# Splitting h into its two float32r parts where it is made, on one Trainium2 core

## The chip, the core and the metric

The kernel is written in the Tile language (dependences, buffer waits and the order of instructions on each engine come from its scheduler) and runs on one NeuronCore of a Trainium2 chip. The metric is the device time of one execution in microseconds (us). TensorE is PE in the rows, its weight loads PEld, VectorE DVE, ScalarE ACT, GpSimd POOL, SyncE SP; SP issues nearly all DMAs, in its own order.

## What is computed

One layer of a hybrid backbone over 2048 latent tokens and 256 context tokens of width 1024. The modulated norm h of all tokens goes through one input projection, whose columns feed three token mixers:

```python
hl = modulate(rms_norm(xl, p["norm_mix_pre"]), ml[0], ml[1])
hc = modulate(rms_norm(xc, p["norm_mix_pre"]), mc[0], mc[1])
qkv_l, z_l, beta_l, alpha_l, lx_l, lg_l, rw_l = split_last(hl @ p["w_in"], IN_SIZES)
qkv_c, z_c, beta_c, alpha_c, lx_c, lg_c, rw_c = split_last(hc @ p["w_in"], IN_SIZES)
```

The mixers are a gated DeltaNet (`gdn`), an RG-LRU (`lru`) and RWKV-7 (`rwk`), each scanned in both directions. Their concatenated outputs go through an output projection, a residual and a squared-ReLU MLP. All is float32. The kernel reaches that accuracy on TensorE with float32r products: an operand x is split into hi = float32r(x) and lo = x - hi, and a product is hi*hi + lo*hi + hi*lo, three matmuls.

## The kernel before

h is made once and kept in DRAM as a float32 tensor `ht` of [128, 8, 2312]: 128 features by 8 groups by the padded tokens. The tokens come in nine pieces of 256 (piece 0 is the context), which overlap by a few columns for the convolutions; a pass over a piece reads 260 columns (`PW`).

`make_h` (L286) makes it, two tiles of 128 tokens to a piece. For each tile x is loaded ("mhx", two buffers), ScalarE squares it into an "mhh" tile (two buffers) to get the row sum, VectorE makes the reciprocal root in some fifteen tiny steps (`rms`), GpSimd scales x (L315), TensorE transposes it in two halves `q` of four 128x128 blocks into PSUM tiles of the tag "rps", ScalarE and VectorE apply scale and shift into the same mhh tile, and SP writes it to `ht` (L328). The pieces come in the order `H_ORDER` = 0, 1, 2, 8, 7, 3, 6, 4, 5. Three are emitted ahead of the RWKV sweep, two in its first piece and one in each of the next four, behind the norm of k (L838).

`Proj.load` (L387) reads a pass: per unit of `u` feature groups a DMA of `ht` into a "hl" tile (L394), a ScalarE cast to hi, "hh" (L397), and a GpSimd subtraction for lo in a second "hl" tile (L398). `Proj.products` (L414) issues the three matmuls (tile "proj"), and `weight` uses the same "hl" ring to stage the weights. There are 54 passes: 9 in the RWKV sweep (u=2, six buffers of each name), 27 in the gated-DeltaNet features (u=2, eight buffers), 9 each in `lru_features` and `gdn_gates` (u=4, three hh and four hl buffers).

The stages: `front` holds make_h and `rwkv_sweep` (L757), which per piece projects 12 column tiles (x3, k, v, r), then for each direction makes decay and in-context rate with small matmuls of the same PSUM tag "rps" (w_up, a_up, evicted as lw and ta), a VectorE scan and products, and writes `pk`. `mixed` weaves the RWKV recurrence with `gdn_features`; `rest` weaves the gated-DeltaNet recurrence with `lru_features`, the LRU, `gdn_gates` and the output projection; `ffn` is last. The program is written in this order, and the scheduler places each engine's instructions by its own model of their times.

Of the kernel before, what the change touches and what calls it, by code (L numbers as in the profile page):

```python
# [7 lines left out]
F32 = mybir.dt.float32  # L8
F32R = mybir.dt.float32r
# [8 lines left out]
KD = 8  # L18
# [4 lines left out]
PW = 260  # L23
# [20 lines left out]
def poff(p):  # L44

    return 0 if p == 0 else 259 + 256 * (p - 1)
# [1 line left out]


SCRATCH = {  # L50
    "ht": ([128, KD, HPAD], F32),
    "modc": ([128, 2, KD], F32),
    "gp2": ([128, D], F32),
    "kq": ([2, 128, NCH, 2, 3, 64], F32),
# [231 lines left out]
def make_h(k, w, pp, tag):  # L286

    d = k.d
    zf = w.tile([128, KD, 4], F32, name="zf", bufs=1)
    k.G.memset(zf, 0.0)  # L290
    k.S.dma_start(out=d["ht"][:, :, 0:2], in_=zf[:, :, 0:2])
    k.S.dma_start(out=d["ht"][:, :, 258:261], in_=zf[:, :, 0:3])
    k.S.dma_start(out=d["ht"][:, :, 2309:2312], in_=zf[:, :, 0:3])

    def load(p):
        xt = []
        for i in range(2):
            t = w.tile([128, D], F32, name="mhx", bufs=2)
            src = d["ctx"][0, 128 * i:128 * i + 128, :] if p == 0 else \
                d["x"][0, 256 * (p - 1) + 128 * i:256 * (p - 1) + 128 * i + 128, :]  # L300
            k.S.dma_start(out=t, in_=src)
            xt.append(t)
        return xt

    for n, p in enumerate(H_ORDER):
        xt = load(p)
        if n == 0:
            yield
        j = 1 if p == 0 else 0
        sc, sh = k.sc[:, j], k.sh[:, j]  # L310
        for i, x in enumerate(xt):
            h = w.tile([128, KD, 128], F32, name="mhh", bufs=2)
            rs = w.tile([128, 1], F32, name="mhs", bufs=6)
            k.act(h.rearrange("p a t -> p (a t)"), x, AF.Square, acc=rs)
            k.ts(k.G, x, x, k.rms(w, rs, D, 1e-6), MUL)  # L315
            for q in range(2):
                ps = pp.tile([128, 4, 128], F32, name="mhps", tag=tag)
                for a in range(4):
                    kk = 4 * q + a
                    k.PE.transpose(ps[:, a, :], x[:, 128 * kk:128 * kk + 128], k.ident)  # L320
                for a in range(4):
                    kk = 4 * q + a
                    if a < 3:
                        k.act(h[:, kk, :], ps[:, a, :], AF.Identity, scale=sc[:, kk:kk + 1], bias=sh[:, kk:kk + 1])
                    else:
                        k.ts(k.V, h[:, kk, :], ps[:, a, :], sc[:, kk:kk + 1], MUL, sh[:, kk:kk + 1], ADD)
            o = poff(p) + 2 + 128 * i
            k.S.dma_start(out=d["ht"][:, :, o:o + 128], in_=h)  # L328
        yield


# [9 lines left out]
class Proj:  # L341


    def __init__(self, k, es, tag, psb=2, u=4, hb=3, raw=4, side="right"):
        self.k, self.u, self.lb, tc = k, u, raw, k.tc
        self.w = es.enter_context(tc.tile_pool(name=tag + "w", bufs=1, side=side))
        self.hp = es.enter_context(tc.tile_pool(name=tag + "h", bufs=hb, side=side))
        self.pp = es.enter_context(tc.tile_pool(name=tag + "p", bufs=psb, space=PSUM, side=side))
        self.nw = 0

    def weight(self, i, c0, m):

        k = self.k
        self.hi[i], self.lo[i] = [self.w.tile([128, KD, m], F32R, name=f"w{x}{i}") for x in ("hi", "lo")]
        n = 2 * self.u
        for q in range(0, KD, n):
            s = slice(q, q + n)
            split(k, (k.V, k.G)[i % 2], k.d["w_in"][0, 128 * q:128 * (q + n), c0:c0 + m].rearrange("(k p) f -> p k f", p=128),
                  self.raw(F32).rearrange("p a t -> p (a t)")[:, 0:n * m].rearrange("p (k f) -> p k f", f=m),
                  self.hi[i][:, s, :], self.lo[i][:, s, :])  # L360

    def raw(self, dtype):

        return self.hp.tile([128, self.u, PW], dtype, name="hl", bufs=self.lb)

    def weights(self, cols):

# [18 lines left out]

    def load(self, p):  # L387

        k = self.k
        out = []  # L390
        o = poff(p)
        for q in range(0, KD, self.u):
            raw, hh, hl = self.raw(F32), self.hp.tile([128, self.u, PW], F32R, name="hh"), self.raw(F32R)
            k.S.dma_start(out=raw, in_=k.d["ht"][:, q:q + self.u, o:o + PW])  # L394
            for a in range(0, self.u, 2):
                x = slice(a, a + 2)
                k.A.copy(hh[:, x, :], raw[:, x, :])  # L397
                k.tt(k.G, hl[:, x, :], raw[:, x, :], hh[:, x, :], SUB)  # L398
            out.append((hh, hl))
        return out  # L400

    def parts(self, f, h, a=0, b=PW):
# [10 lines left out]

    def products(self, ps, f, h, kk, a, b):  # L414

        hh, hl = h[kk // self.u]
        m = self.hi[f].shape[2]
        for n, (w, x) in enumerate(((self.hi[f], hh), (self.hi[f], hl), (self.lo[f], hh))):
            self.k.mm(ps[0:m, 0:b - a], w[:, kk, :], x[:, kk % self.u, a:b], kk == 0 and n == 0, kk == KD - 1 and n == 2)

    def feats(self, fs, h, a=0, b=PW):

# [48 lines left out]
def gdn_features(k, es, sm):  # L471

    d, tc, V, A, G = k.d, k.tc, k.V, k.A, k.G
    cw = k.pc["gdn_conv"]
    c4 = lambda v: v.rearrange("p r (n t) -> p r n t", t=64)
    pj = Proj(k, es, "g", u=2, hb=8, raw=8)
    w = es.enter_context(tc.tile_pool(name="gfw", bufs=2, side="right"))
    gt = chain(gates(k), decays(k, sm))
    rest = ada_rest(k, es.enter_context(k.tc.tile_pool(name="adr", bufs=1, side="right")), sm, "sm")

    def rows(p, y, a):
        to_rows(k, sm, w, d["kv"][0, :, 4 * p:4 * p + 4, a, :], y, "gsq")

    def normed(p, y, sq, s):

        scale = 64.0 if s else 1.0
        k.table("natural_log_exp_and_others")
        for a, b in ((0, 2), (2, 3)):
# [12 lines left out]
        if s == 0:  # L501
            k.tt(G, y, y, sq, MUL)
            rows(p, y, 0)
            yield

    before = None
    tiles = lambda c: [(c + 128 * j, 128) for j in range(3)]
    for s, p, h in pj.passes([tiles(GW) + [(C_BA, 24)], tiles(0), tiles(2 * GW)]):
        next(rest, None)
        y = w.tile([128, 3, 256], F32, name="gy")  # L510
        f0 = (3, 0, 6)[s]
        for j in range(3):
            ps = yield from pj.parts(j, h)
            k.act(y[:, j, :], ps[:, 0:256], AF.Copy, scale=cw[:, f0 + j:f0 + j + 1])
            for tap in range(1, 4):
                k.stt(y[:, j, :], ps[:, tap:tap + 256], cw[:, 9 * tap + f0 + j:9 * tap + f0 + j + 1], y[:, j, :], MUL, ADD)
            yield
        if s == 0:
            ps = yield from pj.parts(3, h, 2, 258)
            b = w.tile([24, 256], F32, name="gba", bufs=1)  # L520
            V.tensor_copy(b, ps[0:24, 0:256])
            k.S.dma_start(out=d["ba"][:, 256 * p:256 * p + 256], in_=b)
        if before:
            yield from normed(*before)
            before = None
        if s > 0:
            next(gt, None)
            next(gt, None)
        k.table("silu_and_others")
        k.act(y, y, AF.Silu)  # L530
        if s < 2:
            sq = w.tile([128, 3, 256], F32, name="gsq", bufs=1)
            k.tt(G, sq, y, y, MUL)
            before = p, y, sq, s
        else:
            rows(p, y, 1)
# [361 lines left out]
def front(k):  # L898

    with ExitStack() as es:  # L900
        pj = Proj(k, es, "r", psb=3, u=2, hb=6, raw=6, side="left")
# [956 lines left out]
```

## Time and profile before

| | us |
|---|---|
| median of 3 runs (lowest to highest) | 4217.18 (4215.35 to 4218.16) |
| profiled execution, own time | 4210.2 |
| its span, first to last instruction | 4208.5 |
| TensorE matmul busy | 3591.0 (85%) |
| VectorE busy | 2424.2 (58%) |
| GpSimd busy | 1672.0 (40%) |
| ScalarE busy | 1574.5 (37%) |
| mean granted TensorE clock, share of full | 0.89 |

Busy time is that of the profiled execution. Matmuls overlap in the array, so a TensorE busy for 90% of a stretch may still have room. "Idle before" of a group of instructions is the time that the engine stood idle just ahead of them, with what ended it. The chain of waits is followed back from the last instruction, at each step to what released it.

### The profile page before, as it was taken

To read this page: it belongs to the slowest core of one execution; us is meant where nothing else is said; L and a number is where in the kernel's file an instruction comes from. 1 tells how busy PE (TensorE), PEld (TensorE's weight loads), DVE (VectorE), ACT (ScalarE), POOL (GpSimd) and SP (SyncE) were. 2 spreads that over 40 slices of the span, in tenths; PEclk is the share of its full clock that TensorE was granted. 3 is DMA by queue.
4 is the path that set the end of the run, shared out by engine and by line. 5 is a ranking of instruction groups with operands and counts; after the bars stand their busy time and mean duration, and the time that the engine had idled before them with its cause. 6 is when DMAs were issued, how large, how long until landed. Compare 5 with 4: busy or idle time off the path is not lost.

```text
span 4208.5 us, 75743 instructions
## 1 busy us (share of the span) xinstructions
PE 3591.0 (85%) x29914; PEld 2997.3 (71%) x29914; DVE 2424.2 (58%) x4389; ACT 1574.5 (37%) x3163; POOL 1672.0 (40%) x1589
## 2 busy tenths in 40 slices
PE   5798995888778867587787689989999999999998
PEld 2777774777667756576675467768888887888886
DVE  3566667766757543299979985643334346333334
ACT  3454443444454532232564445532222222211212
POOL 3333334444465543355585645322232214212212
PEclk8998996788988777788798679999999999999999
DMA  7433335344555644543454556631212123111112
GB/s 207 126 110 121 117 110 170 108 136 135 163 158 158 179 125 148 148 123 110 133 164 146 159 174 186 202 116 46 66 57 62 56 73 125 55 46 46 54 42 85
DMA packets 491798, 499.09 MB, mean 119 GB/s; under 512 B 38819, under 2 KB 443956, under 8 KB 491444
## 3 DMA queue, kind: packets, MB, share of 16 engines
q1 hardware_dynamic: 477620, 471.18, 37.6%
q0 software_dynamic: 5120, 16.78, 1.4%
q10 hardware_dynamic: 8704, 6.29, 0.5%
q8 instruction: 237, 3.88, 0.4%
q14 instruction: 117, 0.96, 0.1%
HBM read 368.45 MB, written 136.30 MB: 120 GB/s over the span
## 4 chain that ended last, share of the span: by engine, by line
PE 50%; DVE 22%; DMA 14%; issue 5%; ACT 5%; POOL 2%; SPq 2%; DVEq 0%; ACTq 0%; POOLq 0%
PE fup L161 16%; PE fdn L161 16%; PE proj L161 6%; PE opm L161 4%; DVE yl L135 3%; DVE ltmp L135 3%; DMA hl<-ht 3%; DMA pk<-pk 3%; PE rps L161 2%; DMA ht<-mhh 2%; DVE ml L1115 1%; DVE pk L135 1%; PE gps L161 1%; DMA dm<-gb 1%; DVE y L1138 1%
## 5 line engine op out<-in xcount | busy, mean ns | idle before, releaser
L161 PE MATMUL proj<-hh,whi 128*128 128x258 f32 (+2 forms) x2040 | 642.4, 318 | 67.0 <-ACT hh L397 17.5
L161 PE MATMUL proj<-hl,whi 128*128 128x258 f32 (+2 forms) x2040 | 627.3, 308 | 3.4 <-POOL hl L135 3.4
L161 PE MATMUL proj<-hh,wlo 128*128 128x258 f32 (+2 forms) x2040 | 623.0, 306 | 0.0
L135 DVE TENSOR_TENSOR facc<-facc,fdn 128x512 f32<-128x512 f32 x480 | 326.3, 686 | 399.0 <-PE fdn L161 399.0
L161 PEld LDWEIGHTS proj<-hh,whi 128*128 128x128 f32 x2040 | 417.3, 206 | 100.4 <-issue 42.1
L161 PEld LDWEIGHTS proj<-hl,whi 128*128 128x128 f32 x2040 | 420.4, 206 | 20.9 <-issue 9.6
L161 PEld LDWEIGHTS proj<-hh,wlo 128*128 128x128 f32 x2040 | 418.7, 206 | 15.9 <-issue 11.3
L135 POOL TENSOR_TENSOR hl<-hl,hh 128x520 fp32r<-128x520 f32 x216 | 296.5, 1379 | 305.1 <-ACT hh L397 235.6
L161 PE MATMUL fup<-fhh,uhi 128*128 128x512 f32 x1024 | 404.5, 395 | 5.7 <-ACT fhh L336 5.7
L161 PE MATMUL fup<-fhl,uhi 128*128 128x512 f32 x1024 | 403.5, 394 | 2.7 <-DVE fhl L135 2.5
L161 PE MATMUL fup<-fhh,ulo 128*128 128x512 f32 x1024 | 403.2, 394 | 0.0
L161 PE MATMUL fdn<-dhi,ah 128*128 128x512 f32 x1024 | 399.7, 391 | 3.8 <-ACT ah L1758 2.0
L161 PE MATMUL fdn<-dlo,ah 128*128 128x512 f32 x1024 | 399.6, 390 | 0.2 <-POOL dlo L135 0.2
L161 PE MATMUL fdn<-dhi,al 128*128 128x512 f32 x1024 | 395.4, 391 | 0.9 <-DVE al L135 0.9
L135 POOL TENSOR_TENSOR dlo<-draw,dhi 128x1024 fp32r<-128x1024 f32 x32 | 77.5, 2422 | 564.2 <-ACT dhi L336 564.2
L336 ACT CAST dhi<-draw 128x1024 fp32r<-128x1024 f32 x64 | 67.1, 1049 | 576.8 <-PE fdn L161 515.0
L135 POOL TENSOR_TENSOR fq<-fr 128x512 f32<-128x512 f32 x128 | 151.8, 1187 | 326.1 <-ACT fr L113 325.4
L397 ACT CAST hh<-hl 128x520 fp32r<-128x520 f32 x216 | 131.3, 623 | 280.9 <-DMA hl<-ht 274.2
L161 PEld LDWEIGHTS fup<-fhh,uhi 128*128 128x128 f32 x1024 | 192.7, 188 | 51.1 <-ACT fhh L336 7.5
L161 PEld LDWEIGHTS fup<-fhl,uhi 128*128 128x128 f32 x1024 | 192.8, 188 | 48.3 <-DVE fhl L135 4.4
L161 PEld LDWEIGHTS fdn<-dhi,ah 128*128 128x128 f32 x1024 | 192.3, 188 | 48.2 <-DVE facc L135 3.0
L135 DVE TENSOR_TENSOR al<-fq,ah 128x512 fp32r<-128x512 f32 x128 | 93.6, 732 | 229.9 <-ACT ah L1758 229.5
(368 smaller groups left out, 7894.8 us busy)
## 6 DMA issues: line engine op xcount, KB each, us to landing
hl<-ht SPq DMA_DIRECT2D x144, 260.0 KB
uraw<-in_ffn_up_dram SPq DMA_DIRECT2D x64, 512.0 KB
draw<-in_ffn_down_dram SPq DMA_DIRECT2D x64, 512.0 KB
pk<-pk SPq DMA_DIRECT2D x18, 1536.0 KB
pk<-pk SPq DMA_DIRECT2D x36, 768.0 KB
hl<-ht SPq DMA_DIRECT2D x36, 520.0 KB
pb<-pk SPq DMA_DIRECT2D x36, 384.0 KB
kqe<-kq SPq DMA_DIRECT2D x72, 192.0 KB
```

Source lines behind the costliest of these rows:

```text
L135: return e.tensor_tensor(out=out, in0=a, in1=b, op=op)
L161: self.last = self.PE.matmul(out, l, r, start=start, stop=stop).ins
L336: k.A.copy(hi, raw)
L397: k.A.copy(hh[:, x, :], raw[:, x, :])
L1115: V.transpose(out=sw(ml[part]), in_=mu[part, :, cc].rearrange("p u i -> p i u"))
L1138: V.transpose(out=y[part, :, cc].rearrange("p u i -> p i u"), in_=sw(yl[part]))
```

## The change

`ht` gets a further axis of two, hi and lo, and its size doubles. make_h now writes each half `q` of a token tile into an mhh tile of its own, [128, 4, 2, 128] float32r (4 KB per partition, as a whole tile had before; still two buffers under one name): the shifted value goes into the lo place, ScalarE copies it rounded into the hi place, GpSimd subtracts in place, and SP writes that half. `Proj.load` becomes one DMA per unit, straight into what the matmuls read; the rings "hh" and "hl" become one ring "hx" of `hb` units of both parts. The matmuls are the same.

```diff
-    "ht": ([128, KD, HPAD], F32),
+    "ht": ([128, KD, 2, HPAD], F32),
...
         for i, x in enumerate(xt):
-            h = w.tile([128, KD, 128], F32, name="mhh", bufs=2)
+            hs = [w.tile([128, 4, 2, 128], F32R, name="mhh", bufs=2)]
             rs = w.tile([128, 1], F32, name="mhs", bufs=6)
-            k.act(h.rearrange("p a t -> p (a t)"), x, AF.Square, acc=rs)
+            k.act(hs[0].bitcast(F32).rearrange("p a b t -> p (a b t)"), x, AF.Square, acc=rs)
             k.ts(k.G, x, x, k.rms(w, rs, D, 1e-6), MUL)
...
+                if q == 1:
+                    hs.append(w.tile([128, 4, 2, 128], F32R, name="mhh", bufs=2))
+                h = hs[q]
+                whole = h[:, :, 1, :].bitcast(F32)
...
-            k.S.dma_start(out=d["ht"][:, :, o:o + 128], in_=h)
+                k.A.copy(h[:, :, 0, :], whole)
+                k.tt(k.G, h[:, :, 1, :], whole, h[:, :, 0, :], SUB)
+                k.S.dma_start(out=ht[:, 8 * q:8 * q + 8, o:o + 128], in_=h.bitcast(F32).rearrange("p k a t -> p (k a) t"))
...
+    def unit(self):
+        return self.hp.tile([128, self.u, 2, PW], F32R, name="hx")
...
         for q in range(0, KD, self.u):
-            raw, hh, hl = self.raw(F32), self.hp.tile([128, self.u, PW], F32R, name="hh"), self.raw(F32R)
-            k.S.dma_start(out=raw, in_=k.d["ht"][:, q:q + self.u, o:o + PW])
-            for a in range(0, self.u, 2):
-                x = slice(a, a + 2)
-                k.A.copy(hh[:, x, :], raw[:, x, :])
-                k.tt(k.G, hl[:, x, :], raw[:, x, :], hh[:, x, :], SUB)
-            out.append((hh, hl))
+            x = self.unit()
+            self.k.S.dma_start(out=x.bitcast(F32).rearrange("p k a t -> p (k a) t"),
+                               in_=self.k.d["ht"][:, q:q + self.u, :, o:o + PW].rearrange("p k a t -> p (k a) t"))
+            out.append(x)
```

## Rows read from the trace of the kernel before

**Rows 1.** busy time of each engine by stage; columns named in the first line

```profile
core 0: us, PE busy (x) PEld busy (x) DVE busy (x) ACT busy (x) POOL busy (x), PEclk, DMA share, GB/s
78.00:631.00 553.00, 483.54 (x3105) 424.61 (x3107) 346.54 (x724) 260.18 (x541) 197.14 (x102) 0.90 0.38 115
631.00:1790.00 1159.00, 866.59 (x11430) 766.36 (x11426) 683.05 (x1247) 494.83 (x975) 534.30 (x549) 0.80 0.51 148
1790.00:2300.00 510.00, 405.30 (x5065) 341.10 (x5063) 458.37 (x870) 227.25 (x471) 310.82 (x350) 0.84 0.47 135
2770.00:4208.00 1438.00, 1413.61 (x6152) 1153.09 (x6152) 580.44 (x799) 338.59 (x565) 375.63 (x279) 0.99 0.21 65
```

**Rows 2.** costliest groups of the page: count, busy us, mean ns, idle before

```profile
L135 POOL TENSOR_TENSOR hl<-hl,hh 128x520 fp32r<-128x520 f32 x216 | 296.5, 1379 | 305.1 <-ACT hh L397 235.6
L135 POOL TENSOR_TENSOR fq<-fr 128x512 f32<-128x512 f32 x128 | 151.8, 1187 | 326.1 <-ACT fr L113 325.4
L397 ACT CAST hh<-hl 128x520 fp32r<-128x520 f32 x216 | 131.3, 623 | 280.9 <-DMA hl<-ht 274.2
```

**Rows 3.** the same stretches, instructions on the tile hl alone

```profile
631.00:1790.00 1159.00, 233.24 (x755) 153.70 (x755) 14.88 (x14) 88.47 (x142) 168.25 (x126) 0.80 0.51 148
1790.00:2300.00 510.00, 136.35 (x430) 91.70 (x429) 3.57 (x2) 38.59 (x65) 92.38 (x66) 0.84 0.47 135
```

**Rows 4.** chain of waits, 631 to 1790 us, shares by line

```profile
by line: DMA hl<-ht 8.0%; PE proj L161 7.9%; DMA pk<-pk 7.3%; issue 6.8%; DVE yl L135 4.9%; DVE ltmp L135 4.8%; DMA dm<-gb 4.3%; PE rps L161 4.0%; PE rbk L161 3.3%; DVE ml L1115 3.0%; DVE gy L143 2.4%; PE rout L161 2.3%; PE rtp L1452 1.9%; 
```

**Rows 5.** timeline 220 to 240 us, SP and GpSimd: start, length, line, engine

```profile
225.87 9.08 SPq L394 DMA_DIRECT2D hl<-ht  x2
...
233.18 1.36 POOL L135 TENSOR_TENSOR hl<-hl,hh 128x520 fp32r<-128x520 f32 x1
```

**Rows 6.** timeline of TensorE, transposes and first decay matmuls of piece 0

```profile
80.09 1.97 PE L320 MATMUL mhps<-ident,mhx 128*128 128x128 f32 x8 [0.80 <-POOL mhx L139]
...
157.74 0.27 PE L320 MATMUL mhps<-ident,mhx 128*128 128x128 f32 x1
157.95 0.70 PE L161 MATMUL rps<-x,rwkv_w_up 64*128 64x256 f32 x2
```

**Rows 7.** timeline of ScalarE, in brackets idle time before and releaser

```profile
72.15 1.06 ACT L113 ACTIVATE mhh<-mhx 128x1024 f32<-128x1024 f32 x1 [7.00 <-DMA ht<-mhh]
...
98.19 0.42 ACT L113 ACTIVATE x<-x 128x256 f32<-128x256 f32 x1 [0.69 <-DVE x L143]
...
163.84 0.47 ACT L113 ACTIVATE lw<-rps,hw 128x256 f32<-128x256 f32 x1
```

**Rows 8.** timeline of SP, issues of h to DRAM

```profile
63.35 1.72 SPq L328 DMA_DIRECT2D ht<-mhh  x2
...
84.30 0.53 SPq L328 DMA_DIRECT2D ht<-mhh  x1
...
107.58 0.53 SPq L328 DMA_DIRECT2D ht<-mhh  x1
...
129.18 0.53 SPq L328 DMA_DIRECT2D ht<-mhh  x1
...
154.92 0.56 SPq L328 DMA_DIRECT2D ht<-mhh  x1
```

**Rows 9.** timeline of GpSimd, scaling of the third token tile

```profile
77.19 2.85 POOL L139 TENSOR_SCALAR mhx<-mhx,rms 128x1024 f32<-128x1024 f32 x1 [10.04 <-DMA hl<-ht]
```

**Rows 10.** waits over the whole span: us in total, times, longest

```profile
ACT mhh L113 <- DMA ht<-mhh: 39.6, 12, 7.0
```

**Rows 11.** chain of waits, 78 to 631 us, shares by line

```profile
by line: PE proj L161 20.5%; DMA ht<-mhh 11.7%; DVE pk L135 9.2%; PE rps L161 6.0%; ACT mhh L113 5.8%; DMA pk<-pk 4.0%; DMA hl<-ht 3.5%; DVE e L143 3.3%; issue 3.3%; DVE rms L143 2.9%; ACT L113 2.8%; DVE pk L143 2.6%; DVE c L864 2.5%; ACT r
```

**Rows 12.** VectorE on yl, 1790 to 2300 us: ns min/median/max, then one shape

```profile
L135 DVE TENSOR_TENSOR ltmp<-yl,ml x150: 143/396/1484, 1795.7 to 2289.1; 128x30 f32<-128x30 f32 x10, 128x58 f32<-128x58 f32 x10, 128x84 f32<-128x84 f32 x10, 128x108 f32<-128x108 f32 x10
...
L135 DVE TENSOR_TENSOR ltmp<-yl,ml 128x30 f32<-128x30 f32 x10 | 4.5, 448 | 0.8 <-issue 0.7
```

More of the change, by code (lines that the diff above doesn't have):

```diff
@@ L288, in make_h @@
     d = k.d
-    zf = w.tile([128, KD, 4], F32, name="zf", bufs=1)
+    zf = w.tile([128, 2 * KD, 4], F32, name="zf", bufs=1)
     k.G.memset(zf, 0.0)
-    k.S.dma_start(out=d["ht"][:, :, 0:2], in_=zf[:, :, 0:2])
-    k.S.dma_start(out=d["ht"][:, :, 258:261], in_=zf[:, :, 0:3])
-    k.S.dma_start(out=d["ht"][:, :, 2309:2312], in_=zf[:, :, 0:3])
+    ht = d["ht"].rearrange("p k a t -> p (k a) t")
+    for o, n in ((0, 2), (258, 3), (2309, 3)):
+        k.S.dma_start(out=ht[:, :, o:o + n], in_=zf[:, :, 0:n])
     def load(p):
@@ L311, in make_h @@
         for i, x in enumerate(xt):
-            h = w.tile([128, KD, 128], F32, name="mhh", bufs=2)
+            hs = [w.tile([128, 4, 2, 128], F32R, name="mhh", bufs=2)]
             rs = w.tile([128, 1], F32, name="mhs", bufs=6)
-            k.act(h.rearrange("p a t -> p (a t)"), x, AF.Square, acc=rs)
+            k.act(hs[0].bitcast(F32).rearrange("p a b t -> p (a b t)"), x, AF.Square, acc=rs)
             k.ts(k.G, x, x, k.rms(w, rs, D, 1e-6), MUL)
+            o = poff(p) + 2 + 128 * i
             for q in range(2):
@@ L323, in make_h @@
                     if a < 3:
-                        k.act(h[:, kk, :], ps[:, a, :], AF.Identity, scale=sc[:, kk:kk + 1], bias=sh[:, kk:kk + 1])
+                        k.act(whole[:, a, :], ps[:, a, :], AF.Identity, scale=sc[:, kk:kk + 1], bias=sh[:, kk:kk + 1])
                     else:
-                        k.ts(k.V, h[:, kk, :], ps[:, a, :], sc[:, kk:kk + 1], MUL, sh[:, kk:kk + 1], ADD)
-            o = poff(p) + 2 + 128 * i
-            k.S.dma_start(out=d["ht"][:, :, o:o + 128], in_=h)
+                        k.ts(k.V, whole[:, a, :], ps[:, a, :], sc[:, kk:kk + 1], MUL, sh[:, kk:kk + 1], ADD)
+                k.A.copy(h[:, :, 0, :], whole)
+                k.tt(k.G, h[:, :, 1, :], whole, h[:, :, 0, :], SUB)
+                k.S.dma_start(out=ht[:, 8 * q:8 * q + 8, o:o + 128], in_=h.bitcast(F32).rearrange("p k a t -> p (k a) t"))
         yield
@@ L341, with __init__ @@
 class Proj:
-    def __init__(self, k, es, tag, psb=2, u=4, hb=3, raw=4, side="right"):
-        self.k, self.u, self.lb, tc = k, u, raw, k.tc
+    def __init__(self, k, es, tag, psb=2, u=4, hb=3, side="right"):
+        self.k, self.u, tc = k, u, k.tc
         self.w = es.enter_context(tc.tile_pool(name=tag + "w", bufs=1, side=side))
@@ L358, in weight @@
             split(k, (k.V, k.G)[i % 2], k.d["w_in"][0, 128 * q:128 * (q + n), c0:c0 + m].rearrange("(k p) f -> p k f", p=128),
-                  self.raw(F32).rearrange("p a t -> p (a t)")[:, 0:n * m].rearrange("p (k f) -> p k f", f=m),
+                  self.unit().bitcast(F32).rearrange("p k a t -> p (k a t)")[:, 0:n * m].rearrange("p (k f) -> p k f", f=m),
                   self.hi[i][:, s, :], self.lo[i][:, s, :])
-    def raw(self, dtype):
-        return self.hp.tile([128, self.u, PW], dtype, name="hl", bufs=self.lb)
+    def unit(self):
+        return self.hp.tile([128, self.u, 2, PW], F32R, name="hx")
     def weights(self, cols):
@@ L387, in load @@
     def load(self, p):
-        k = self.k
         out = []
@@ L414, in products @@
     def products(self, ps, f, h, kk, a, b):
-        hh, hl = h[kk // self.u]
+        x = h[kk // self.u][:, kk % self.u]
         m = self.hi[f].shape[2]
-        for n, (w, x) in enumerate(((self.hi[f], hh), (self.hi[f], hl), (self.lo[f], hh))):
-            self.k.mm(ps[0:m, 0:b - a], w[:, kk, :], x[:, kk % self.u, a:b], kk == 0 and n == 0, kk == KD - 1 and n == 2)
+        for n, (w, i) in enumerate(((self.hi[f], 0), (self.hi[f], 1), (self.lo[f], 0))):
+            self.k.mm(ps[0:m, 0:b - a], w[:, kk, :], x[:, i, a:b], kk == 0 and n == 0, kk == KD - 1 and n == 2)
     def feats(self, fs, h, a=0, b=PW):
@@ L475, in gdn_features @@
     c4 = lambda v: v.rearrange("p r (n t) -> p r n t", t=64)
-    pj = Proj(k, es, "g", u=2, hb=8, raw=8)
+    pj = Proj(k, es, "g", u=2, hb=8)
     w = es.enter_context(tc.tile_pool(name="gfw", bufs=2, side="right"))
@@ L900, in front @@
     with ExitStack() as es:
-        pj = Proj(k, es, "r", psb=3, u=2, hb=6, raw=6, side="left")
+        pj = Proj(k, es, "r", psb=3, u=2, hb=6, side="left")
         pss = es.enter_context(k.tc.tile_pool(name="rss", bufs=3, space=PSUM))
```

## Prediction

> **What bounds the kernel now.** I read the busy time by stage first [rows 1]. Four stages follow one another: the RWKV sweep (78 to 631 us, "front"), the RWKV recurrence woven with the gated-DeltaNet features (631 to 1790, "mixed"), the gated-DeltaNet recurrence with the LRU and gate features (1790 to 2300 and on, "rest"), and the feed-forward part from 2770, where TensorE is busy for 98% and which the diff does not touch. Only front, mixed and rest read h. In front and mixed no engine is full: TensorE 87% and 75%, VectorE 63% and 59%. There the order of events counts, so I read the chain of waits next. In rest VectorE is busy for 90%.
>
> What the change takes aim at: 216 casts on ScalarE and 216 subtractions on GpSimd, 131 and 297 us [rows 2]. In mixed they are 88 and 168 us, in rest 39 and 92 us (both rows count some weight splits too) [rows 3]. Neither engine is a bound there, so these sums are no gain by themselves. What can be gained is what lies on the chain: in mixed the load of h holds 8.0% of the chain, 93 us [rows 4].
>
> **Part 1: make_h, where a split and a buffer rule are added.** Per 128 tokens it gains two ScalarE copies and two GpSimd subtractions of 128x512, 36 of each. The nearest row for the subtraction is 1.19 us (fq), for the copy 0.62 us (the cast of 128x520) [rows 2]: 43 and 22 us. The sweep loses its own 36 of each, 49 and 22 us, so front's engine sums stay as they are.
>
> The buffers do not. Before, a token tile held one "mhh" buffer from its Square until its DMA had landed, and the two buffers let two tiles run together. Now a tile takes both buffers in turn. The second of a pair can start its Square only when the first half of the tile ahead has landed.
>
> This hangs on whether tiles of one name get their buffers strictly in program order. Two readings say they do. In the sweep, the second load of a pair is blocked for 9 us and goes out when the subtraction of the first is done, though of the six buffers four hold the running pass and one the first load, so one was free: it was kept for that subtraction's result [rows 5]. And the first decay matmuls (w_up) of piece 0 had their input at 98.6 us, yet ran at 157.95, straight behind the last transposes of the tenth token tile, which share their PSUM name; ScalarE took them up at 163.84 [rows 6, 7].
>
> So the tenth tile's transposes set when piece 0 can go on. Before, pairs of tiles were issued at 63, 84, 108, 129 and 155 us: 22.9 us for a pair, the time that a buffer is held [rows 8]. One hold worked out: the Square starts the moment a DMA lands (72.15, which is 8.8 us after its issue), GpSimd scales at 77.19 for 2.85, the transposes follow at 80.09, ScalarE and VectorE take some 4 us to the DMA at 84.30 [rows 6 to 9]. After, a hold has half of the transposes and evictions (about 2 us less) and a copy and a subtraction in their place (about 2 us more), so 21 us, between 18.6 (no queueing) and 22.9. But it now serves one tile. The second tile takes the place in time of the third, transposes at 80, and the tenth follows eight holds later: 80 + 8 x 21 = 248, between 229 and 263, where it was 157.7. **Loss 90 us (71 to 105).** It is on the path: piece 1's norm waits for a buffer that piece 0's decay part frees, and so on through the pieces.
>
> Each of the next four pieces also makes two tiles inside its own chain. The second now waits for the first half's landing, Square, norm, scaling and transposes: about 17 us where ScalarE already waited some 7 us for landings (12 such waits, 39.6 us in all, longest 7.0) [rows 10]. I take 8 us for four pieces, **32 us (0 to 48)**.
>
> On the other side the sweep's loads hold 3.5% of front's chain, 19 us [rows 11], and with twice the units in the ring and no cast behind them I take back **15 us (0 to 23)**. The next late thing is the decay chain itself. Front: +90 + 32 - 15 = **+107 us** (+55 to +150).
>
> **Part 2: the loads.** Each pass reads 8 x 128 x 2 x 260 x 4 bytes, 2.13 MB in place of 1.065, 54 times: +57.5 MB, and 9.4 MB more are written. The issues stay four or two per pass, on SP, past the same neighbours. In mixed 27 passes add 28.8 MB. The DMA engines moved 148 GB/s at a share of 0.51 [rows 1], so 290 at full share, and 28.8 MB are 99 us of all engines: the share goes to 0.60. Other DMA waits on mixed's chain, pk<-pk 7.3% and dm<-gb 4.3% [rows 4], are 134 us; lengthened in proportion that costs 23 us, hidden it costs nothing; I take 15.
>
> **Part 3: mixed without casts.** ScalarE no longer stands in line behind a DMA and GpSimd behind ScalarE, and the eight units hold two passes, so a load has a whole pass as its cover. If that cover fails, the wait moves to TensorE, with all recurrence matmuls behind it. Of the 93 us I take 56, since the loads of pk and dm come late right behind; with 10 us for freed ScalarE and GpSimd time: 15 - 56 - 10 = **-51 us** (-110 to +25).
>
> **Part 4: rest.** VectorE is the bound, and the trace shows it stretched: the fastest subtraction product (ltmp, the smallest shape) took 143 ns, the mean of that same shape is 448 [rows 12]. Over the 300 such instructions, 0.2 us each make 60 us; GpSimd was busy for 311 us, 92 of them the subtractions that go, or 30% [rows 1, 3]. So 20 us come back (0 to 45). Against it, three units of half of h each hold one and a half passes, and the second half waits for TensorE; up to 15 us. **-20 us** (-45 to +15).
>
> The Trainium skill, SBUF - State Buffer, section "SBUF: two separate sides", says that VectorE with two SBUF inputs and a GpSimd operation that reads SBUF lock each other out of a shared port for the whole instruction. The stretch just read agrees in kind.
>
> **Sum.** 107 - 51 - 20 = +36 us on the profiled execution, 4210.2 us (span 4208.5 and 1.7 around it): 4246. The median of the runs stands 7 us above it: **4253 us**.
>
> **Rivals.**
> - *Full lock-out* (faster): if every removed subtraction had blocked VectorE for its own length whenever VectorE was busy, 0.90 x 92 in rest and 0.59 x 168 in mixed [rows 1, 3] give 83 and 99 us in place of 20 and 10: 4253 - 152 = 4101. VectorE is not the bound in mixed, so at most half: about 4175. This is the page's rule taken strictly. Chance 0.12, with a short front loss in the same case.
> - *The second tile gets a buffer early* (faster): then both tiles go on together, a hold of half a tile and one of a whole share two buffers, 15 us per tile. Ten tiles end near 200, most of it under PE work that was late anyway; front loses about 15 us: 4160. Against it: rows 5 to 7. Chance 0.20.
> - *Cancelling*: front 75, mixed and rest -70: 4217 within 8. Chance 0.10.
> - *The loads stay late* (slower still): SP's loads wait in order behind other DMAs of the weave and the second pass of units is never filled, while double transfers lengthen pk and dm: mixed gives 0 to +25, 4304 to 4329. It decides when a load lands later than one pass after its issue. Its ground is that SP is shared: the load already waited in line [rows 5]. Chance 0.10.
>
> **How the numbers follow.** Forecast (slower, front's loss larger than mixed's and rest's gains) 0.48, the others as given. Faster by over 0.2% (8 us, about what a measurement can tell): 0.20 + 0.12 = 0.32; within: 0.10; slower: 0.48 + 0.10 = 0.58. The likeliest case alone spans 4226 to 4310. The range of 4165 to 4315 leaves out half of the early-buffer case and half of the late-load case.
>
> **What would show it.** Right: the gaps between ht<-mhh issues in the first 250 us come in twos (two halves) every 20 us, the w_up matmuls of piece 0 start near 250 us, the mixed stage begins near 730 and is 40 to 60 us shorter than 1159, hl<-ht gone from its chain. Wrong: tiles still in pairs, or w_up before 200 us; mixed shorter by over 100 us; VectorE's small products back near 143 ns in rest.

## The result and the profile after

The changed kernel takes 4238.31 us (median of 4 runs, 4235.04 to 4242.42) where the kernel before took 4216.27 us beside it (4211.88 to 4218.16): 1.0054 of before, 95% interval 1.0037 to 1.0072. It is slower by half a per cent. The profiled execution of after spans 4233.3 us, that of before 4208.5 us: 24.8 us more.

To see where these 25 us come from I cut both traces at the same four events: the last write of the RWKV sweep (pk), the last step of the gated-DeltaNet features (gy), the last eviction of the gate (z), and the first copy of the feed-forward accumulator (facc). Timelines of single tiles, kernel before; behind the colon min/median/max in ns, then the start of the first and of the last instruction in us:

```profile
L884 SPq DMA_DIRECT2D pk<-pk x18: 359/360/1389, 189.6 to 670.4; - x18
L143 DVE SCALAR_TENSOR_TENSOR gy<-proj,parB,gy x243: 462/483/486, 708.5 to 1724.4; 128x256 f32<-128x256 f32 x122
L568 ACT COPY z<-proj x24: 349/372/377, 2049.9 to 2276.6; 128x256 f32<-128x256 f32 x24
L1812 DVE COPY facc<-fdn x32: 680/692/693, 2801.8 to 3543.5; 128x512 f32<-128x512 f32 x32
```

The same four of after:

```profile
L888 SPq DMA_DIRECT2D pk<-pk x18: 359/365/1968, 264.2 to 787.0; - x18
L144 DVE SCALAR_TENSOR_TENSOR gy<-proj,parB,gy x243: 375/484/486, 813.8 to 1790.6; 128x256 f32<-128x256 f32 x122
L572 ACT COPY z<-proj x24: 348/372/376, 2048.9 to 2295.9; 128x256 f32<-128x256 f32 x24
L1816 DVE COPY facc<-fdn x32: 682/692/693, 2827.1 to 3568.5; 128x512 f32<-128x512 f32 x32
```

| Stretch | before | after | difference |
|---|---|---|---|
| front, to the last pk | 670.4 | 787.0 | +116.6 |
| mixed, to the last gy | 1054.0 | 1003.6 | -50.4 |
| rest, to the last z | 552.2 | 505.3 | -46.9 |
| to the first facc | 525.2 | 531.2 | +6.0 |

Front loses more than mixed and rest gain together. Behind the first facc both traces run 1406 us.

In front, the stores of h now come in twos, the two halves of one token tile, 17 to 27 us apart, where before one of a pair of tiles came every 21 to 26 us [rows 8]. SP in the timeline of after (start, length, line, operation, count):

```profile
88.58 1.58 SPq L336 DMA_DIRECT2D ht<-mhh  x2
112.67 1.61 SPq L336 DMA_DIRECT2D ht<-mhh  x2
131.63 1.60 SPq L336 DMA_DIRECT2D ht<-mhh  x2
...
251.03 1.58 SPq L336 DMA_DIRECT2D ht<-mhh  x2
```

TensorE in the same trace shows the tenth tile's transposes and the first decay matmul right behind them, at 247.63 us instead of 157.95 [rows 6]:

```profile
245.73 1.97 PE L322 MATMUL mhps<-ident,mhx 128*128 128x128 f32 x8 [15.93 <-POOL mhx L140]
247.63 1.82 PE L162 MATMUL rps<-x,rwkv_w_up 64*128 64x256 f32 x3
```

The waits of the whole span (us in total, times, longest) show what came of the waits for h. Before, ScalarE's casts stood for 274.2 us in front of loads [rows 2]; after, TensorE itself waits 47.1 us for them. ScalarE's wait for a tile of h to land in DRAM has grown from 39.6 us [rows 10] to 71.0:

```profile
ACT mhh L114 <- DMA ht<-mhh: 71.0, 15, 9.7
PE proj L162 <- DMA hx<-ht: 47.1, 8, 16.4
```

Busy time by stage, same stretches and columns as [rows 1]:

```profile
78.00:631.00 553.00, 367.56 (x2335) 321.61 (x2336) 259.75 (x608) 218.07 (x444) 163.10 (x85) 0.79 0.49 122
631.00:1790.00 1159.00, 938.00 (x11933) 832.35 (x11931) 722.70 (x1376) 473.69 (x943) 391.21 (x416) 0.83 0.58 175
1790.00:2300.00 510.00, 397.17 (x5239) 341.27 (x5240) 405.83 (x859) 199.31 (x419) 242.14 (x312) 0.86 0.65 198
```

From 78 to 631 us TensorE does only 2335 matmuls where it did 3105: front is late, not busier. In the third stretch VectorE falls from 458.37 to 405.83 us with about as many instructions, and the DMA share rises from 0.47 to 0.65.

### The profile page after: what moved, and what is told of

The parts are those of the page before. It is cut to its first block, busy times and chain, and to the rows that moved or that the text cites. A ratio compares the mean times of both kernels' runs of the same rounds, so it can differ in the third digit from the quotient of the medians.

```text
span 4233.3 us, 75399 instructions
## 1 busy us (share of the span) xinstructions
PE 3553.3 (84%) x29914; PEld 2971.8 (70%) x29914; DVE 2344.8 (55%) x4389; ACT 1487.1 (35%) x2987; POOL 1434.1 (34%) x1409
## 5 line engine op out<-in xcount | busy, mean ns | idle before, releaser
L162 PE MATMUL proj<-hx,whi 128*128 128x258 f32 (+2 forms) x4080 | 859.5, 307 | 101.5 <-DMA hx<-ht 47.1
L162 PEld LDWEIGHTS proj<-hx,whi 128*128 128x128 f32 x4080 | 678.7, 201 | 145.3 <-issue 59.5
L162 PE MATMUL proj<-hx,wlo 128*128 128x258 f32 (+2 forms) x2040 | 611.8, 301 | 0.0
L162 PEld LDWEIGHTS proj<-hx,wlo 128*128 128x128 f32 x2040 | 409.4, 201 | 10.1 <-issue 5.8
L162 PEld LDWEIGHTS fup<-fhh,ulo 128*128 128x128 f32 x1024 | 193.0, 188 | 44.6
L162 PEld LDWEIGHTS fdn<-dhi,al 128*128 128x128 f32 x1024 | 192.2, 188 | 41.6 <-DVE al L136 0.8
L162 PEld LDWEIGHTS fdn<-dlo,ah 128*128 128x128 f32 x1024 | 192.3, 188 | 41.2
L144 DVE SCALAR_TENSOR_TENSOR gy<-proj,parB,gy 128x256 f32<-128x256 f32 x243 | 115.2, 479 | 160.9 <-ACT gy L114 149.4
```

Of the source, the lines that this page charges most:

```text
L144: return self.V.scalar_tensor_tensor(out=out, in0=a, scalar=s, in1=b, op0=op0, op1=op1)
L162: self.last = self.PE.matmul(out, l, r, start=start, stop=stop).ins
```

## The experiments

All of them were timed on other chips than the pair above, four in all; the kernel before takes 4197 to 4200 us on each. Below, a ratio is always to the kernel before on the same chip. Stretches are cut at the events of the table, in one profiled execution of each kernel; the stretches of the kernel before were not taken on these chips, and the kernel before with half blocks (ratio 0.9997, below) stands for it.

### Is it the hold of the mhh buffers, or what the split adds?

Theory: front loses because one hold of the buffers now serves one token tile instead of two. Rival: it loses by the copies, the subtractions and the doubled bytes. The first test takes the kernel before, without any split, and gives it the fault alone:

```diff
-            h = w.tile([128, KD, 128], F32, name="mhh", bufs=2)
+            h = w.tile([128, KD, 128], F32, name="mhh", bufs=1)
```

> The kernel before with one buffer instead of two for the tile of h that make_h fills (mhh), nothing else: no split, no doubled bytes, no extra copy or subtraction. Theory A (the front loses because a hold of the mhh buffers, from the Square that opens it to the landing of its store, now serves one tile instead of two): this kernel has the same fault by other means, so its ten tiles come one per hold of 19 to 25 us; the first matmul of w_up comes at 220 to 250 us instead of 157.9, and the time is 75 to 115 us above before, 4291 to 4331 us. Rival B (the front loses by what the split adds: a copy, a subtraction and twice the bytes for each tile): none of that is in here, the first w_up matmul stays within 10 us of 157.9 and the time within 15 us of before.

Measured: 4309.17 us, ratio 1.0258 (1.0241 to 1.0276), 110.5 us over before. The ten stores come one by one, 15 to 24 us apart (SP in the timeline of this kernel):

```profile
94.80 0.53 SPq L328 DMA_DIRECT2D ht<-mhh  x1
114.51 0.53 SPq L328 DMA_DIRECT2D ht<-mhh  x1
129.89 0.59 SPq L328 DMA_DIRECT2D ht<-mhh  x1
```

The first decay matmul comes at 223.65 us, again right behind the transposes of the tenth tile:

```profile
221.76 1.97 PE L320 MATMUL mhps<-ident,mhx 128*128 128x128 f32 x8 [13.88 <-POOL mhx L139]
223.65 2.73 PE L161 MATMUL rps<-x,rwkv_w_up 64*128 64x256 f32 x5
```

The last pk comes at 791.8 us. On these chips it comes at 652.1 us in the kernel before with half blocks and at 772.9 in the changed kernel, so a kernel with no split at all loses as much in front as the changed one, and 19 us more; theory A holds. The first decay matmul in those two kernels (TensorE):

```profile
150.68 0.70 PE L161 MATMUL rps<-x,rwkv_w_up 64*128 64x256 f32 x2
239.65 3.29 PE L162 MATMUL rps<-x,rwkv_w_up 64*128 64x256 f32 x6
```

Up to this point one buffer alone brings 73 of the 89 us. The other 16 are not explained by it; what the split adds to each hold is the likely place.

The second test goes the other way: keep the split and let two tiles be in flight again. That needs 4 KB of SBUF per partition, so a control had to be made first, which frees it elsewhere:

```diff
-        pj = Proj(k, es, "r", psb=3, u=2, hb=6, side="left")
+        pj = Proj(k, es, "r", psb=3, u=2, hb=5, side="left")
...
-                w = p.tile([128, KD, 512], F32, name="adawt")
+                w = [p.tile([128, 4, 512], F32, name="adawt", bufs=7) for _ in range(2)]
```

> A control for the two that follow: the changed kernel with 5 instead of 6 units in the ring of the first sweep and with the first modulation's weights in half blocks (7 tiles instead of 4 double ones), which frees the room that the others need. Both theories expect the time of the changed kernel, 4238 us, within 15 us, and the first w_up matmul at 240 to 255 us; a shallower ring may cost up to 20 us in the sweep, and what it costs is to be taken off the next two.

Measured: 4156.45 us, ratio 0.9900 (0.9883 to 0.9916), with the first decay matmul at 240.45 us. Front is as forecast (last pk at 772.4), but the kernel is 1.5% faster than expected, in stages that were not edited. That has a section of its own below. On the control:

```diff
-            hs = [w.tile([128, 4, 2, 128], F32R, name="mhh", bufs=2)]
+            hl = w.tile([128, KD, 128], F32R, name="mhh", bufs=2)
...
+                hi = w.tile([128, 4, 128], F32R, name="mhi", bufs=2)
+                lo = hl[:, 4 * q:4 * q + 4, :]
+                whole = lo.bitcast(F32)
```

> The control with the buffers of make_h laid out so that two tiles are in flight again: the whole tile (which becomes the low part in place) is one 4 KB buffer of two, as before the change, and the high part of each half tile has a ring of its own of two 2 KB buffers. Same copies, subtractions and bytes, four stores per tile instead of two. Theory A (one tile per hold costs the front): the first w_up matmul comes at 160 to 185 us, the front gets back 65 to 95 us, and the time is 4140 to 4175 us plus what the control costs, less than before by 1 to 2%. Rival B (the copy, the subtraction and the doubled bytes cost it): the first w_up matmul stays at 235 to 255 us and the time is the control's within 15 us.

Measured: 4129.92 us, ratio 0.9827 (0.9814 to 0.9841). Two tiles run together again; their stores interleave (SP) and the first decay matmul comes at 180.42 us, 60 us earlier than in the control (TensorE):

```profile
98.68 0.36 SPq L335 DMA_DIRECT2D ht<-mhh  x1
100.28 0.58 SPq L335 DMA_DIRECT2D ht<-mhh  x1
105.60 1.96 SPq L335 DMA_DIRECT2D ht<-mhh  x2
122.94 0.92 SPq L335 DMA_DIRECT2D ht<-mhh  x1
```

```profile
180.42 0.70 PE L162 MATMUL rps<-x,rwkv_w_up 64*128 64x256 f32 x2
```

The last pk comes at 682.3 us, 90.1 us before the control's. The kernel gains only 26.5 us over the control, because the later stages, which have the same work, give back 66: mixed takes 984.5 us against 959.2, the stretch from z to facc 554.0 against 516.2, rest 501.6 against 498.6. So theory A is borne out in front, at the upper end of its 65 to 95 us, while the time of the whole is not what either theory said.

Third, what in the hold is long? The Square of a tile writes values that nobody reads, into the buffer that it thereby opens. Given a small buffer of its own, on the control:

```diff
-            k.act(hs[0].bitcast(F32).rearrange("p a b t -> p (a b t)"), x, AF.Square, acc=rs)
+            k.act(w.tile([128, D], mybir.dt.bfloat16, name="mhq", bufs=1), x, AF.Square, acc=rs)
```

> The control with the Square of a tile writing a 2 KB buffer of its own (its values are used by nobody, only its sum is) instead of the first half's mhh buffer. A hold of an mhh buffer then begins at the transposes and leaves out the Square, the row statistics on DVE and the scaling on GpSimd, some 8 us of the 19 to 20 us. Theory A, with the Square as what opens the hold: a tile's halves follow each other at 8 to 12 us, the first w_up matmul comes at 165 to 205 us, and the time is 40 to 85 us under the control. Rival C (the hold is made of the transposes, evictions, split and landing, and the Square is only early by the way): first w_up at 235 to 255 us and the control's time within 15 us.

Measured: 4102.03 us, ratio 0.9766 (0.9753 to 0.9780), 54 us under the control: the fastest kernel of this study. The first tiles follow each other 12 to 15 us apart and the first decay matmul comes at 173.19 us; the last pk at 667.6 us is 104.8 us before the control's. The later stages give back 61 us of that against the control, 47 of them in mixed (1005.9 us against 959.2).

```profile
83.23 1.58 SPq L336 DMA_DIRECT2D ht<-mhh  x2
95.59 1.59 SPq L336 DMA_DIRECT2D ht<-mhh  x2
108.74 8.91 SPq L336 DMA_DIRECT2D ht<-mhh  x3
...
173.19 1.09 PE L162 MATMUL rps<-x,rwkv_w_up 64*128 64x256 f32 x2 [0.89 <-DVE mhh L141]
```

### Why the control was faster than the changed kernel

Theory O: the scheduler lays out the instructions of all stages anew for every edit, and one order is better than another. Rivals: the chip (P), the half-block weight loads (Q), the shallower ring itself (R). The changed kernel was run again, and each of the control's edits alone:

> The changed kernel as it is, beside the three that follow on one chip. The control with five ring units and half-block weight loads took 0.990 of before where the changed kernel took 1.0054 of it, though only the front should have felt its edits. Theory O (the control's gain is real: the order in which the build lays the instructions of the mixed stage is made anew for every edit, and one order is some tens of us better than another): this kernel stands at 1.004 to 1.007 of before again. Rival P (the chip or the day): it comes out within 0.3% of the control, 0.987 to 0.993.

> The changed kernel with the first modulation's weights in half blocks alone (seven tiles of 8 KB instead of four of 16 KB). By theory Q (the weight loads are what the control gained by) the first w_up matmul comes at 238 to 243 us and the ratio to before is 0.988 to 0.994. By theory R (the shallower ring) it is 1.000 to 1.008, as the changed kernel. By theory O it may be anything from 0.985 to 1.015, with a mixed stage (last eviction of the sweep to last eviction of the features) that is longer or shorter by up to 50 us than the 1046 us of the changed kernel without a word in it that was edited.

> The changed kernel with five instead of six units in the ring of the first sweep alone. By theory R the ratio to before is 0.988 to 0.994, with the first w_up matmul at 240 to 248 us; by theory Q it is 1.003 to 1.010, as fewer units can only make the sweep's loads later; by theory O anything from 0.985 to 1.015, most of the difference in the mixed stage.

> The kernel before with the first modulation's weights in half blocks, the edit that stands in the controls. Theory Q: it gains as the control gained, 0.985 to 0.992 of before. Theory R or a gain that only the changed kernel can have: 0.997 to 1.003. Theory O: 0.985 to 1.015, and the stage where the difference lies is not the one that was edited.

| Kernel | ratio to before (95%) | front | mixed | rest | z to facc |
|---|---|---|---|---|---|
| changed, again | 1.0064 (1.0046 to 1.0082) | 772.9 | 1004.4 | 502.4 | 530.2 |
| + half blocks | 1.0056 (1.0041 to 1.0071) | 767.3 | 1006.4 | 503.7 | 532.5 |
| + ring of 5 | 1.0019 (1.0009 to 1.0029) | 775.5 | 967.2 | 494.4 | 546.8 |
| + both (control) | 0.9900 (0.9883 to 0.9916) | 772.4 | 959.2 | 498.6 | 516.2 |
| before + half blocks | 0.9997 (0.9987 to 1.0007) | 652.1 | 1051.0 | 550.5 | 529.6 |

The changed kernel stands where it stood. The control was timed on another chip than the other four rows; the kernel before takes 4198.63 us there and 4197.03 on theirs, and the kernel with the Square apart, timed beside the control, has the mixed stage of the changed kernel (1005.9 us). So the chip is an unlikely cause. The half blocks alone are out: they move neither kernel. The ring alone brings 1.0019, not the 0.988 to 0.994 of theory R. It takes 37 and 47 us off mixed, a stage in which that ring no longer exists, and changes the stretch from z to facc by +17 and -16 us. Laid side by side, the instruction streams of the traces show what the ring did change: behind front, 1142 and 1020 of VectorE's some 3540 instructions would have to move to turn one order into the other, against 125 for the half blocks in the changed kernel and none for the half blocks in the kernel before. In mixed, four executions have the same order of VectorE: the changed kernel twice, with half blocks, and with the subtractions put back in rest (below). They take 1003.6 to 1006.4 us on three chips. So a new order goes with these differences and an unchanged one with none. That the order causes them is likely but not shown: no run changed the order alone.

This gives every other comparison its measure: where an edit reorders a stage, 16 to 47 us of that stage's time may be the order, as in this table. Mixed took 1051.0 and 1067.3 us in the two kernels without the split on these chips, and 959.2 to 1006.4 in seven kernels with it and with nothing else edited there. Its gain is therefore more than the order, though its size carries the order in it.

### Where rest gained

Theory A: GpSimd's subtractions slowed VectorE's small operations. In the changed kernel the subtractions were put back in rest alone, off every path:

```diff
+            if self.u == 4:
+                for a in range(0, self.u, 2):
+                    j = self.hp.tile([128, 2, PW], F32, name="hj", bufs=1)
+                    y = x[:, a:a + 2].bitcast(F32)
+                    self.k.tt(self.k.G, j, y[:, :, 1, :], y[:, :, 0, :], SUB)
```

> The changed kernel with the subtractions of h put back on GpSimd in the passes of the stage rest alone: 72 of 128x520, as before, from the loaded parts into a buffer that nobody reads, so the loads, the products and ScalarE keep what the change gave them. Theory A (the stage rest gained because GpSimd's subtractions had slowed VectorE's small operations by holding what both share on the way to SBUF): the mean of ltmp in the stage goes back from 424 to 490 to 540 ns, VectorE's busy time there from 402 to 430 to 450 us, and the stage grows by 20 to 45 us, the time by as much: ratio 1.011 to 1.017 of before. Rival B (the gain came from loads that are there sooner, or from ScalarE's casts that are gone, or from the order): ltmp stays under 450 ns, the stage within 10 us, the ratio at 1.004 to 1.009.

Measured: 4272.96 us, ratio 1.0171 (1.0157 to 1.0185), 45 us over the changed kernel (1.0064). Rest takes 550.6 us, as before the change (550.5), and mixed 1006.3, as in the changed kernel. VectorE's costliest groups in rest (busy us, mean ns, idle before), first the changed kernel, then this one:

```profile
L136 DVE TENSOR_TENSOR yl<-yl,ltmp 128x30 f32<-128x30 f32 (+9 forms) x143 | 61.0, 427 | 2.4
L136 DVE TENSOR_TENSOR ltmp<-yl,ml 128x30 f32<-128x30 f32 (+9 forms) x143 | 60.6, 424 | 2.6
L1119 DVE STREAM_TRANSPOSE ml<-mu 32x1024 f32<-32x1024 f32 (+1 forms) x15 | 32.9, 2190 | 0.3
L136 DVE TENSOR_TENSOR s<-gps,colt 64x192 f32<-64x192 f32 x72 | 25.6, 355 | 8.4 <-PE gps L162 6.7
```

```profile
L136 DVE TENSOR_TENSOR ltmp<-yl,ml 128x30 f32<-128x30 f32 (+9 forms) x145 | 85.0, 586 | 2.3
L136 DVE TENSOR_TENSOR yl<-yl,ltmp 128x30 f32<-128x30 f32 (+9 forms) x144 | 68.6, 476 | 2.5
L1124 DVE STREAM_TRANSPOSE ml<-mu 32x1024 f32<-32x1024 f32 (+1 forms) x15 | 32.9, 2192 | 0.3
L136 DVE TENSOR_TENSOR s<-gps,colt 64x192 f32<-64x192 f32 x72 | 25.6, 355 | 2.6 <-PE gps L162 0.9
```

The first two groups, with two inputs in SBUF, take 32 us more; the transposes, with one input, and the products that read PSUM take the same time. VectorE in the whole stretch takes 450.69 us against 401.69. GpSimd's subtractions of 128x520 cost rest its whole gain, though GpSimd bounds nothing there, a little more than theory A's ranges on all counts.

The loads and the casts are out for rest, since this kernel keeps what the change did to them. The order is not quite the same: 168 of VectorE's some 846 instructions in rest would have to move. But in the nine kernels without these subtractions rest takes 494 to 506 us, whatever their order, and in the four with them 528 to 552. An order can be worth some 20 us there, not the 48.

### Where mixed gained

Two things changed there: the loads no longer pass ScalarE and GpSimd, with a ring that reaches a pass further; and ScalarE and GpSimd got 59 and 143 us of time back (first and last of the four rows below; the 88 and 168 us of [rows 3] hold weight splits too). First their work was put back, on loaded units but into buffers that nobody reads:

```diff
+            if self.u == 2 and self.nq:
+                y = x.bitcast(F32)
+                for a in range(2):
+                    j, m = [self.hp.tile([128, 216], F32, name=n, bufs=1) for n in ("hj", "hm")]
+                    self.k.A.copy(j, y[:, a, 0, 0:216])
+                    self.k.tt(self.k.G, m, y[:, a, 1, 0:216], y[:, a, 0, 0:216], SUB)
```

> The changed kernel with work put back on ScalarE and GpSimd in the stage mixed, but off the path of the loads: for each of the 108 loaded units, two copies on ScalarE and two subtractions on GpSimd of 128x216 elements (83% of what the change removed, in twice as many instructions) into buffers that nobody reads. Theory A (mixed gained because the conversion left the path from the load to the matmul and the ring reaches a pass further): the stage stays within 15 us of the changed kernel's 1004 us, the ratio within 0.003 of 1.006. Rival B (mixed gained because ScalarE and GpSimd became free and VectorE with them): the stage goes back to 1030 to 1055 us and the ratio to 1.012 to 1.018. The order of the stage can move either by some 20 us.

Measured: 4276.42 us, ratio 1.0175 (1.0156 to 1.0194). Then the ring of mixed was cut to 5 units:

> The changed kernel with 5 units instead of 8 in the ring of the features in the stage mixed. A pass takes four, so the loads of the next pass now wait for the matmuls of the present one, as the eight small buffers made them before the change. Theory A (the deeper reach of the ring is where mixed gained): the waits of matmuls for hx loads, 1 us in the changed kernel, grow to 20 us and more and the stage by 20 to 60 us, the ratio to 1.011 to 1.020. Rival B (freed engines): the stage stays within 15 us of 1004 us and the ratio within 0.003 of 1.006.

Measured: 4244.11 us, ratio 1.0108 (1.0090 to 1.0125). The stage mixed by its window, columns as in [rows 1]: the changed kernel, the work put back, the short ring, and the kernel before with half blocks:

```profile
772.90:1777.30 1004.40, 796.00 (x10974) 709.52 (x10974) 612.36 (x1199) 404.27 (x804) 337.03 (x374) 0.83 0.59 178
770.30:1840.60 1070.30, 824.64 (x10975) 735.73 (x10974) 637.57 (x1199) 474.54 (x1020) 478.97 (x590) 0.80 0.55 167
770.30:1800.30 1030.00, 816.08 (x10974) 723.81 (x10974) 612.86 (x1199) 409.10 (x812) 341.26 (x388) 0.82 0.58 174
652.10:1703.10 1051.00, 805.22 (x10974) 716.96 (x10974) 648.19 (x1199) 463.38 (x912) 479.72 (x482) 0.83 0.49 142
```

TensorE's waits for h in the same stage (us in total, times, longest), work put back and short ring; in the changed kernel it is 1.0 us:

```profile
PE proj L162 <- DMA hx<-ht: 1.8, 2, 1.0
PE proj L162 <- DMA hx<-ht: 37.5, 11, 9.2
```

With the work back on ScalarE and GpSimd, mixed takes 1070 us, more than before the change, though the loads reach TensorE as early as ever. (GpSimd is then as busy as before the change, ScalarE 11 us more.) So the freed engines are worth as much as the whole gain, and theory A of that run falls. The short ring costs 26 us and brings 37.5 us of waits for h: the deeper reach is needed as well. The two do not add up: of the 47 us that mixed gained on these chips none are left with the work back, and 21 with the short ring. Both edits also gave mixed a new order, 243 and 251 of VectorE's 1198 instructions. The 66 us are more than any order was seen to be worth; the 26 us are not, and for them the waits alone speak.

How does work on engines that are not full cost 66 us? VectorE is busy for 25 us more (637.57 against 612.36, the stretch that rest showed), so about 25 us may be its part. A second part can be seen on ScalarE, whose copies wait for loads; in this place what stands behind them then runs without a gap, so it had probably been ready and waiting too (ScalarE in the timeline of the run with the work put back; in brackets the idle time before and what ended it):

```profile
1161.54 0.78 ACT L407 COPY hj<-hx 128x216 f32<-128x216 f32 x2 [4.29 <-DMA hx<-ht]
1163.02 0.78 ACT L407 COPY hj<-hx 128x216 f32<-128x216 f32 x2 [0.71 <-DMA hx<-ht]
1163.70 2.44 ACT L114 ACTIVATE adw<-adw,cs 128x128 f32<-128x128 f32 x8
1166.16 0.48 ACT L1463 COPY kbn<-rtp 128x384 f32<-128x384 f32 x1
```

The last run was meant to price that waiting, by letting the same work read units that a load a pass earlier had fetched:

```diff
-            if self.u == 2 and self.nq:
...
+        if self.nq:
+            for x in self.old:
...
+            self.old = out
```

> The kernel with put-back work in the stage mixed, with one thing changed: the two copies and two subtractions of 128x216 elements read the units that the call of load before had fetched, so their data has landed a pass earlier and neither ScalarE nor GpSimd sits in front of a load (104 units instead of 108, as the last ones are not read). In the run before, ScalarE's copies had 139 us of idle time ahead of them that ended with a load, GpSimd's subtractions 159 us, and the stage took 1070 us against 1004 us. Theory A (the conversion cost the stage by waiting: a copy that waits for its load holds up all that stands behind it on its engine): the idle time before the copies falls under 40 us, and the stage falls to 1004 to 1035 us, ratio 1.005 to 1.011. Rival B (the conversion cost by its work: engine time, and VectorE's small operations that it slows): the stage stays at 1050 to 1075 us, ratio 1.014 to 1.020, with ltmp and yl at 460 to 490 ns and VectorE's busy time at 630 us or more. VectorE's part alone, its 25 us of more busy time, would be the same under both.

Measured: 4270.94 us, ratio 1.0176 (1.0155 to 1.0196), mixed 1072.2 us. It did not do what it was for. The idle time of ScalarE ahead of the copies, by what ended it, is the same in the run with the work put back and in this one:

```profile
  DMA hx<-ht: 139.2, 67
```

```profile
  DMA hx<-ht: 136.4, 61
```

The scheduler put the copies back to where they had been: of the instructions behind front that both runs have, two of VectorE's and one of ScalarE's stand in another order than in the run before. Neither theory is tested by it; it only repeats the 1070 us. How the 66 us divide between VectorE's stretch, waiting in line and order stays open; the 41 us beyond VectorE's longer busy time have no measured owner.

## Why the prediction was right, step by step

The forecast of 4253 us, slower, was 15 us high; the measured difference is +22 us where +36 was the sum. The direction came out for the reason given: front loses more than mixed and rest gain. That the total came so near owes something to luck, since front was 10 us over its term, rest gained 27 us more than its own, and 6 us came where none were forecast.

**Front, +107 forecast, +116.6 measured.** The main term is right in place and size: tenth tile's transposes forecast at 248 us, seen at 245.73, the first decay matmul 89.7 us later than before against 90. The first store is issued at 71.06 us and the tenth at 251.03, 20.0 us for a hold where 21 was forecast. (The range of 55 to 150 for front is a little narrower than the ends of its parts, 48 to 153, and its hold of 18.6 us stands on no row.) The reading that buffers of one name go out in program order [rows 5 to 7] carried it, and the kernel with one buffer and no split shows the mechanism by itself. What follows it, +32 - 15 = +17 forecast, came to 27. Part of this probably has a cause that I had not named: on GpSimd the sweep's product kd stands behind the scaling of the token tiles (GpSimd and TensorE in the timeline of after).

```profile
327.82 6.50 POOL L140 TENSOR_SCALAR mhx<-mhx,rms 128x1024 f32<-128x1024 f32 x1 [3.48 <-PE proj L162]
336.05 1.80 POOL L136 TENSOR_TENSOR kd<-kd,kx 128x768 f32<-128x768 f32 x1
342.96 2.93 PE L162 MATMUL rps<-kd,ork 128*128 128x256 f32 x6 [9.87 <-POOL kd L136]
```

TensorE's waits for kd from the first decay matmul to the last pk are 3.8 us before, 49.9 us in five waits in the changed kernel and 65.4 in the kernel with one buffer, but 12.9 with two tiles in flight and 16.3 with the Square apart.

**Mixed, -51 forecast, -50.4 measured.** The sum is right, its split is not, so the agreement is partly luck: an order alone was worth up to 47 us in this stage. I gave 56 us to loads that leave the chain and 10 to freed engines. With the loads as they are now and the engines loaded again, the stage is at 1070 us and nothing is left of the gain; with the engines free and the ring short, 26 us are lost. What went wrong is that I read hl<-ht's 8.0% of the chain [rows 4] as lateness of the load, to be priced apart from the engines. The runs show that the two prices do not add; that other work stood behind ScalarE's waits for the load is likely, but its price was not measured. The doubled bytes (15 us in the sum) were not tested by themselves. The DMA share in the stage rose to 0.59 where 0.60 was forecast, and TensorE's waits for pk there from 24.6 to 38.5 us, which is of the size of that term.

**Rest, -20 forecast, -46.9 measured.** The mechanism was named, the size was not: I gave the subtractions their 30% of GpSimd's time as their share of a 60 us stretch. Putting the subtractions back costs 48.2 us of the stage (502.4 to 550.6), and VectorE 49 us of busy time. The 60 us were read from the 300 ltmp products and yl sums, at 0.2 us each where the row of the smallest shape has 0.3 [rows 12], and these carry 32 of the 49 us, over half of the 60 instead of 30%. The other 17 us lie in instructions that I had not counted, products of the LRU among them. The end of the range, 45 us, was passed by 2.

The Trainium skill, SBUF — State Buffer, section "SBUF: two separate sides", would have a VectorE instruction with two SBUF inputs and a GpSimd instruction that reads SBUF lock each other out for their whole length. The run with the subtractions put back agrees: its 72 subtractions take 97.7 us and cost VectorE 49, in products with two SBUF inputs above all, while the transposes and the products that read PSUM keep their length. My rival took the rule as one for all of VectorE's busy time and set 83 us for rest. In the changed kernel the instructions with two SBUF inputs fill about 223 of the 502 us of rest, and that share of 97.7 us is 43 us: a rough estimate, but near the 49 measured. So the rival's size fails, and not the rule.

**The stretch from z to facc, +6.0**, was not in the forecast; by the control runs an order can move it by more than that.

**The rivals.** That the second tile gets a buffer early is out: the stores come in twos and the first decay matmul at 247.6 us. That the loads stay late is out for mixed, 1.0 us of waits. It does hold in small at the start of the sweep, where TensorE waits 31.5 us for two loads before 247 us, in the shadow of the holds. Cancelling would have needed a front loss of 75 us.

## What to carry to other kernels

When a change splits one buffer into two of the same name, count how many units of work are then in flight, and follow one hold from the instruction that opens it to the landing that ends it. An output that nobody reads should not open such a hold: giving the Square a buffer of its own, with the control's edits, took the kernel from 1.0056 (half blocks alone) to 0.9766 of before. Front is 99.7 us shorter between these two, and each later stage lies within 8 us. Work on an engine that bounds nothing can still be what slows the bound, through the engine beside it and, it seems, by standing in line for a load; and before a difference of 1% is put down to a mechanism, look whether the instructions of an unedited stage have been reordered.

## What was not expected of the hardware and the order

Subtractions of 128x520 on GpSimd, 1.36 us each, lengthen VectorE's 128-partition products beside them from a mean of 424 to 586 ns in rest, while the products of 64x192 that read PSUM (s<-gps) stay at 355 ns and the transposes (ml<-mu) at 2190 ns in both runs. A reordering of unedited stages went with up to 47 us in one stage, and with 1.5% of the kernel: more than the change itself moved. That the order is the cause was not shown.
